# S5 outputs stored and fetched by GpSimd's queue, octaves 2 and 3 mixed behind more products

## The chip, the cores and the metric

The kernel runs on one NeuronCore of one Trainium2 chip. The metric is the device time of one execution in microseconds (us), lower is better; a kernel's time is the median over its runs. Engine names are those of the profile: PE is TensorE (matmuls), PEld its weight loads, DVE is VectorE, ACT is ScalarE, POOL is GpSimd, SP is SyncE. SPq and POOLq are the instruction queues of SP and POOL from which DMAs are issued.

## What is computed

One encoder layer over 512 tokens of width 1024, in float32. The part that matters here is the parallel mixer: an S5 state-space branch and a gMLP branch, merged by gates.

```python
xa, zu, zv = proj[..., :512], proj[..., 512:1536], proj[..., 1536:2560]
gate_a, gate_b = sigmoid(proj[..., 2560:3584]), sigmoid(proj[..., 3584:])
y  = d * u + s5_scan(u, forward) + s5_scan(u, backward)   # 32 groups of 16 channels, 64 states
y  = gelu(y)
ya = y * sigmoid(y @ w_glu)                               # 512 x 512
yb = gelu(zu) * spatial_mix(layer_norm(gelu(zv)))
merged = gate_a * (ya @ w_proj_a) + gate_b * (yb @ w_proj_b)
h = h + merged @ w_out
# then memory cross-attention and a SwiGLU feed-forward, unchanged here
```

## The kernel before

Each float32 product is made of three matmuls on a rounded high part and a remainder (`mm3`): high by high, low by high, high by low. A weight block of 512 KB is loaded by SP into a raw buffer (`wraw`, three buffers), rounded by ACT into `whi` (line 85) and subtracted by DVE into `wlo` (line 86), three buffers each. `next_w` takes the blocks in the order of a plan; it starts loads three blocks ahead and splits two blocks ahead. The raw buffer is free when `wlo` is written, and SP's next load waits for that.

The products with `w_proj_b` (`b_product`, line 1158) follow a scheme of seven half-size products for each half n of the columns, so fourteen blocks are used, each with 24 matmuls. They are written out by hand in lines 1223 to 1275, in accumulators `bx`, `bq`, `x1` and their copies (`seed`, `kept`). In the text, product (n, q) is product q of half n.

The S5 branch is a side program. Its 32 groups form four octaves of eight groups. `s5_outputs(o)` copies the scanned states of octave o to `ss`, and after a while `mix_` runs 24 matmuls, 48 records in the trace, into `py` (line 948): taps `tt` by inputs `u`, and output matrices `e` by states `ss`. DVE copies `py` to `yn` (957), PE transposes it to `pyt` (963), and DVE copies that to `y` (968). The matrices of octaves 2 and 3 were spilled to DRAM earlier (`ed`, `kd`) and are fetched back when the mix of octave o-2 is done (`reload`): SP loads `e` (867), POOL's queue loads `tt` (860).

How far such a step is put behind the one before it is set with `later(n, fn)`: `tick(us)` after each product counts work in units of 5.2 us, and what is due is then emitted. The emitted program is then ordered by a scheduler with a cost model; instructions marked `in_order` keep their place.

`store_outputs(n)` takes up to n finished octaves: ACT applies the gelu to `y` in place (980), and two DMAs for each octave write `y` to the DRAM scratch `yd[o]` (983), transposing its layout. After product (1,6) the S5 pool is closed; the pool `merge` takes its place, and a small memset `pad` on POOL (line 130) is the first to write there, so it waits for all users of the old pool. Then `ygt` is loaded from `yd` (1262), split into `yg_hi` on ACT (1263) and `yg_lo` on DVE (1264), and after the last two products the product with `w_glu` (`pf<-yg_hi` in line 360) begins.

Of the kernel before, what the change touches and what calls it, by code (L numbers as in the profile page):

```python
# [9 lines left out]
F32 = mybir.dt.float32  # L10
F32R = mybir.dt.float32r
AF = mybir.ActivationFunctionType
ALU = mybir.AluOpType
# [39 lines left out]
def hybrid_layer_kernel(  # L53
# [8 lines left out]
    nc = tc.nc  # L62
# [14 lines left out]
    def bank(name):  # L77
        return pm.tile([P, 512], F32, tag="mm", name=name)

    def aux(name, shape=(P, 512)):  # L80
        return pa.tile(list(shape), F32, tag="aux", name=name)
# [11 lines left out]
    in_order = tc.keep_in_program_order  # L93
# [349 lines left out]
    def later(n, fn):  # L443

        side["later"].append((side["now"] + n, fn))
# [171 lines left out]
    yd = [dp.tile([GO * C, Q, NCH], F32, name=f"yd{o}") for o in range(NO)]  # L617
# [163 lines left out]
    def lc(t, g):  # L781
        return t[:, g].rearrange("p a b -> p (a b)")
# [70 lines left out]
    ed = {o: dp.tile([2, P, GO * Q * C], F32, name=f"ed{o}") for o in (2, 3)}  # L853
# [10 lines left out]
    def reload(o):  # L864
        es = [s5p.tile([P, GO, Q, C], F32, tag="e%d" % i, name="e%d" % i, bufs=2) for i in range(2)]
        for i, e in enumerate(es):
            nc.sync.dma_start(glc(e), ed[o][i])
        load(o, es)
# [56 lines left out]
    def s5_outputs(o):  # L925
        gs = slice(o * GO, (o + 1) * GO)
        while ("oct", o) not in st:
            yield None
        e_re, e_im, tt = st["oct", o]
        zh, u = st["zh"], st["u"]  # L930
        ss = s5p.tile([P, 2, GO, NCH], F32, tag="wt", name="ss", bufs=2)
        zv = zh[:, :, :, gs].rearrange("p n i g -> p i g n")
        nc.gpsimd.memset(ss[lo_, :, :, 0:1], 0.0)
        nc.gpsimd.memset(ss[hi_, :, :, NCH - 1:NCH], 0.0)
        nc.scalar.copy(ss[lo_, :, :, 1:NCH], zv[lo_, :, :, 0:NCH - 1])
        V.tensor_copy(ss[hi_, :, :, 0:NCH - 1], zv[hi_, :, :, 0:NCH - 1][:, :, :, ::-1])

        def mix_():
            ps = aux("py", (P, 4, 2, 4, C))
            ks = (0, 1, 2) if o in ed else (1, 2, 0)  # L940
            for h in range(4):
                for k in ks:
                    for j in range(2):
                        g = 4 * j + h
                        a = u[:, o * GO + g, :] if k == 0 else ss[:, k - 1, g, :]
                        b = (lc(e_re, g), lc(e_im, g))[k - 1].rearrange("p (d q c) -> p d q c", d=2, q=4) if k else \
                            tt[:, h].rearrange("p (d q j c) -> p j d q c", d=2, q=4, j=2)[:, j]
                        in_order(nc.tensor.matmul(ps[64 * j:64 * j + 64, :, :, h, :].rearrange("p q d c -> p d q c"), a,
                                                  b, start=k == ks[0], stop=k == ks[2], tile_position=(0, 64 * j)))
            later(1, lambda: emit(ps))  # L950
            if o + 2 in ed:
                later(0.5, lambda: reload(o + 2))

        def emit(ps):

            y = s5p.tile([P, 512], F32, tag="etmp", name="yn")
            V.tensor_copy(y, ps.rearrange("p q d g c -> p (q d g c)"))
            later(0.5, lambda: turn_y(y))

        def turn_y(y):  # L960
            ps = aux("pyt", (P, 2, 4, NCH))
            for q in range(4):
                in_order(nc.tensor.transpose(ps[:, :, q, :], y[:, q * P:(q + 1) * P], ident))
            later(0.5 if o else 1.5, lambda: put(ps))

        def put(ps):
            y = s5p.tile([P, 512], F32, tag=("y", "bbr", "bbi", "raw_b")[o], name="y")
            V.tensor_copy(y, ps.rearrange("p s q n -> p (s q n)"))
            st["ys"].append((o, y))

        later(1, mix_)
        yield 5.0

    st["ys"] = []
# [1 line left out]
    def store_outputs(n):  # L976

        ready, st["ys"] = st["ys"][:n], st["ys"][n:]
        for o, y in ready:
            in_order(nc.scalar.activation(y, y, AF.Gelu_apprx_tanh))  # L980
            ydo = yd[o].rearrange("(s f) (d q) n -> d f s (q n)", s=2, d=2)
            for d in range(2):
                nc.sync.dma_start(ydo[d], y[64 * d:64 * d + 64].rearrange("p (s r) -> p s r", s=2))

    def s5_program():
        yield from s5_setup()
        for o in (2, 3):
            yield from s5_kernels(o)
        while "u" not in st:
            yield None  # L990
        zh = s5p.tile([P, NCH, 2, G], F32, name="zh")
        st["zh"] = zh
        for o in range(NO):
            yield from s5_inputs(o)
        for o in (0, 1):
            yield from s5_kernels(o)
        while st.get("nz", 0) < 2 * NO:
            yield None
        yield None
        yield from s5_scan()  # L1000
        for _ in range(2):
            yield None
        for o in range(NO):
            yield from s5_outputs(o)
# [161 lines left out]
    def unit_bank(name):  # L1166
        return bank(name).rearrange("p (j t) -> p j t", j=2)

    def seed(x):
        v = unit_bank("qv")  # L1170
        nc.scalar.copy(v, x)
        return v

    def kept(x, name):
        t = np_.tile([P, 2, 256], F32, tag="ev", name=name, bufs=2)
        nc.scalar.copy(t, x)
        return t

    def minus(x, t):
        nc.vector.tensor_tensor(t, x, t, ALU.subtract)  # L1180
        return t
# [17 lines left out]
    def last_sum(i):  # L1199
        k, lw, z0 = slice(2 * i, 2 * i + 2), slice(2 * i + 4, 2 * i + 6), zf[i][:, :, T0]  # L1200
        for yb_ in yb:
            nc.vector.tensor_tensor(z0, z0, yb_[:, lw, T0].bitcast(F32), ALU.add)
        split(bops[3][0][:, k], bops[3][1][:, k], z0)
# [14 lines left out]
    def gated(n, f, ts, src):  # L1218

        dst = part[:, 4 * n + 2 * f:4 * n + 2 * f + 2, ts]  # L1220
        nc.vector.tensor_tensor(dst, src, dst, ALU.mult)
# [7 lines left out]
    b_product(bv, 0, 2)  # L1229
    gated(0, 0, T0, bv)  # L1230
    store_outputs(2)
    b_product(bx, 0, 6)
    u2 = kept(bx, "u2")
    store_outputs(2)
    x1 = unit_bank("bx")
    b_product(x1, 1, 1, True)
    v1 = seed(x1)
    for i in range(2):
        last_sum(i)
    b_product(bx, 0, 7)  # L1240
    u3 = kept(bx, "u3")
    b_product(v1, 1, 2)
    gated(1, 0, T0, v1)
    gated(0, 1, T1, minus(bq, u3))
    b_product(bx, 0, 4)
# [3 lines left out]
    nc.scalar.copy(u1, x1)  # L1249
    finish_side()  # L1250
    store_outputs(NO)
    s5.close()
    mgx = ExitStack()
# [4 lines left out]
    yg_hi = mgp.tile([P, 4, T], F32R, name="yg_hi")  # L1258
    yg_lo = mgp.tile([P, 4, T], F32R, name="yg_lo")
    ygt = mgp.tile([P, 4, T], F32, name="ygt")  # L1260
    for m in range(4):
        nc.sync.dma_start(ygt[:, m, :], yd[m].rearrange("p l n -> p (l n)"))
        in_order(nc.scalar.copy(yg_hi[:, m, :], ygt[:, m, :]))
        nc.vector.tensor_tensor(yg_lo[:, m, :], ygt[:, m, :], yg_hi[:, m, :].bitcast(F32), ALU.subtract)
    b_product(bq, 0, 3)
    gated(0, 1, T0, minus(bq, u2))
    b_product(x1, 1, 7)
    u3 = kept(x1, "u3")
    bq = unit_bank("bq")
    b_product(bq, 1, 5, True)  # L1270
    gated(1, 1, T1, minus(bq, u3))
# [594 lines left out]
    for i in range(2):  # L1866
        p = aux("pcut", (P, 256))
# [37 lines left out]
```

## Time and profile before

| | |
|---|---|
| median of 3 runs | 874.87 us (873.5 to 876.44) |
| profiled execution: its own time | 879.31 us |
| its span, first to last instruction | 877.5 us |
| PE busy | 861.4 us of the span |
| DVE, ACT, POOL busy | 661.0, 464.9, 84.2 us |
| mean granted TensorE clock | 0.995 |
| DMA rate over the span | 193 GB/s moved by the core's 16 DMA engines |

Rows of the timeline give start, duration, engine, line, operation, output and inputs; in brackets stands the idle time of the engine before it and what ended that. A row of `xN` covers N instructions that follow each other. "To landing" is the time from the issue of a DMA until its semaphore shows it done. The profiled execution is one execution and lies above the three timed runs.

### The profile page before, as it was taken

How to read it: one execution, taken by the hardware profiler on the slowest of the kernel's cores; microseconds unless marked ns; L12 is line 12 of the kernel's file. 1: busy time of each engine (PE TensorE's matmuls, PEld its weight loads, DVE VectorE, ACT ScalarE, POOL GpSimd, SP SyncE). 2: the span in 40 equal slices, each digit the busy share in tenths (PEclk: the TensorE clock that was granted, in tenths of full speed). 3: DMA queues.
4: the chain of work that ended last, by engine and by line, in shares of the span. 5: the costliest groups of instructions: out<-in, count | busy, mean ns of one | idle time of the engine just before them, and what ended most of it. 6: DMA issues, size and time to landing. Idle time of an engine off the chain costs nothing.

```text
span 877.5 us, 14737 instructions
## 1 busy us (share of the span) xinstructions
PE 861.4 (98%) x5766; PEld 767.3 (87%) x5766; DVE 661.0 (75%) x1072; ACT 464.9 (53%) x693; POOL 84.2 (10%) x115
## 2 busy tenths in 40 slices
PE   7999999999999999999999999999999999999997
PEld 5787888888888988889899887999999999988885
DVE  5599895989846677658857746767878767899875
ACT  5543864144355553547556544645455454655674
POOL 1002100301020001100001001101111111000010
PEclk8999999999999999999999999999999999999999
DMA  8769656797653898736677546536899898366563
GB/s 243 191 164 293 132 156 179 170 251 193 168 168 95 271 310 253 248 107 208 202 236 220 133 124 169 164 126 171 226 238 224 218 240 217 97 181 212 195 229 107
DMA packets 116488, 169.56 MB, mean 193 GB/s; under 512 B 9265, under 2 KB 81473, under 8 KB 116290
## 3 DMA queue, kind: packets, MB, share of 16 engines
q1 hardware_dynamic: 96450, 140.59, 49.0%
q0 software_dynamic: 19680, 27.50, 19.7%
q8 instruction: 45, 0.74, 0.3%
q10 hardware_dynamic: 288, 0.52, 0.2%
q14 instruction: 25, 0.20, 0.1%
HBM read 159.71 MB, written 48.73 MB: 238 GB/s over the span
## 4 chain that ended last, share of the span: by engine, by line
PE 88%; DMA 6%; DVE 3%; ACT 1%; issue 1%; SPq 1%; ACTq 0%; DVEq 0%
PE pf L360 26%; PE pt L360 16%; PE px L1158 12%; PE pq L1158 6%; PE dx L360 5%; PE dq L360 3%; PE pv L1158 3%; PE qx L1158 2%; PE dv L360 2%; PE pz L892 2%; DMA wraw<-bsum 2%; DMA e<-ed 1%; PE psc L360 1%; PE ptr L520 1%; PE qq L1158 1%; DMA slab<-in_s_log_step_dram 1%
## 5 line engine op out<-in xcount | busy, mean ns | idle before, releaser
L85 ACT CAST whi<-wraw 128x1024 fp32r<-128x1024 f32 (+1 forms) x145 | 148.6, 1025 | 155.9 <-PE pf L360 54.7
L86 DVE TENSOR_TENSOR wlo<-wraw,whi 128x1024 fp32r<-128x1024 f32 (+1 forms) x145 | 172.1, 1189 | 61.1 <-ACT whi L85 60.5
L360 PE MATMUL pf<-xn,whi 128*128 128x512 f32 x448 | 140.3, 392 | 0.0
L360 PEld LDWEIGHTS pf<-xn,whi 128*128 128x128 f32 x448 | 83.7, 188 | 17.5 <-issue 0.4
L360 PE MATMUL pf<-xn,wlo 128*128 128x512 f32 x224 | 87.6, 392 | 0.0
L1158 PE MATMUL px<-fn,whi 128*128 128x256 f32 x480 | 83.3, 276 | 0.0
L1158 PEld LDWEIGHTS px<-fn,whi 128*128 128x128 f32 x480 | 72.5, 188 | 0.2
L86 DVE TENSOR_TENSOR wlo<-b,whi 128x1024 fp32r<-128x1024 f32 x40 | 48.9, 1223 | 26.0 <-ACT whi L85 25.9
L85 ACT CAST whi<-b 128x1024 fp32r<-128x1024 f32 x40 | 42.1, 1054 | 48.5 <-PE px L1158 27.4
L1158 PE MATMUL px<-fn,wlo 128*128 128x256 f32 x240 | 66.4, 277 | 0.0
L1158 PE MATMUL pq<-s,whi 128*128 128x256 f32 x320 | 55.0, 276 | 0.0
L360 PE MATMUL dx<-whi,s 128*128 128x512 f32 x166 | 52.2, 391 | 0.4 <-DVE h L1829 0.4
L86 DVE TENSOR_TENSOR wlo<-t,whi 128x1024 fp32r<-128x1024 f32 x30 | 36.7, 1225 | 18.4 <-ACT whi L85 18.4
L85 ACT CAST whi<-t 128x1024 fp32r<-128x1024 f32 x30 | 31.6, 1054 | 34.3 <-PE pv L1158 11.4
L360 PEld LDWEIGHTS pf<-xn,wlo 128*128 128x128 f32 x224 | 42.1, 188 | 8.7 <-issue 0.2
L1158 PEld LDWEIGHTS pq<-s,whi 128*128 128x128 f32 x320 | 48.2, 188 | 0.0
L360 PE MATMUL pt<-whi,xn 128*128 128x512 f32 x128 | 45.3, 421 | 2.4 <-ACT xn L85 2.1
L1158 PEld LDWEIGHTS px<-fn,wlo 128*128 128x128 f32 x240 | 45.1, 188 | 0.0
L1158 PE MATMUL pq<-s,wlo 128*128 128x256 f32 x160 | 44.2, 276 | 0.0
L360 PEld LDWEIGHTS dx<-whi,s 128*128 128x128 f32 x166 | 31.1, 188 | 7.4 <-issue 0.8
L360 PEld LDWEIGHTS pt<-whi,xn 128*128 128x128 f32 x128 | 25.0, 198 | 9.0 <-ACT xn L85 2.8
L360 PE MATMUL dx<-wlo,s 128*128 128x512 f32 x83 | 32.3, 391 | 0.0
(454 smaller groups left out, 2198.8 us busy)
## 6 DMA issues: line engine op xcount, KB each, us to landing
wraw<-in_w_in_dram SPq DMA_DIRECT2D x36, 512.0 KB, 4.6
dsum<-in_w_down_dram SPq DMA_DIRECT2D x20, 512.0 KB, 6.3
wraw<-dsum SPq DMA_DIRECT2D x20, 512.0 KB, 3.9
b<-in_w_gate_dram SPq DMA_DIRECT2D x15, 512.0 KB, 5.4
b<-in_w_up_dram SPq DMA_DIRECT2D x15, 512.0 KB, 5.3
wraw<-in_w_down_dram SPq DMA_DIRECT2D x15, 512.0 KB, 4.2
dsum<-in_w_down_dram POOLq DMA_DIRECT2D x10, 512.0 KB, 8.2
dsum<-dsum POOLq DMA_DIRECT2D x10, 512.0 KB, 8.0
```

The lines of the kernel that those rows point to most:

```text
L85: hi = nc.scalar.copy(dst_hi, src)
L86: lo = nc.vector.tensor_tensor(dst_lo, src, dst_hi.bitcast(F32), ALU.subtract)
L360: m = nc.tensor.matmul(ps, a[x], b[y], start=start and i == 0, stop=stop and i == 2, skip_group_check=free)
L520: m = nc.tensor.transpose(ps[:, j, :], src[:, k * P:(k + 1) * P], ident)
L892: nc.tensor.matmul(ps[:, g, :], wt[:, g, :], u[:, o * GO + g, :], start=True, stop=True)
L1158: nc.tensor.matmul(ps[:, j, :], a[x], b[y], start=start and j == k == i == 0, stop=k == 3 and i == 2, skip_group_check=True)
```

## The change

Four edits. The mix of octaves 2 and 3 is emitted 2.6 units after the copies to `ss`, not 1. The eight stores to `yd` and the four loads of `ygt` are issued by POOL's queue, not SP's. The second call of `store_outputs(2)` becomes two calls with one octave each, after the seed of product (1,1) and after product (1,2). The split of `ygt` into `yg_hi` and `yg_lo` is emitted after product (1,7), no longer right behind the loads.

```diff
-        later(1, mix_)
+        later(2.6 if o in ed else 1, mix_)
         yield 5.0
...
             for d in range(2):
-                nc.sync.dma_start(ydo[d], y[64 * d:64 * d + 64].rearrange("p (s r) -> p s r", s=2))
+                nc.gpsimd.dma_start(ydo[d], y[64 * d:64 * d + 64].rearrange("p (s r) -> p s r", s=2))
...
     u2 = kept(bx, "u2")
-    store_outputs(2)
     x1 = unit_bank("bx")
     b_product(x1, 1, 1, True)
     v1 = seed(x1)
+    store_outputs(1)
     for i in range(2):
         last_sum(i)
     b_product(bx, 0, 7)
     u3 = kept(bx, "u3")
     b_product(v1, 1, 2)
+    store_outputs(1)
...
     for m in range(4):
-        nc.sync.dma_start(ygt[:, m, :], yd[m].rearrange("p l n -> p (l n)"))
-        in_order(nc.scalar.copy(yg_hi[:, m, :], ygt[:, m, :]))
-        nc.vector.tensor_tensor(yg_lo[:, m, :], ygt[:, m, :], yg_hi[:, m, :].bitcast(F32), ALU.subtract)
+        nc.gpsimd.dma_start(ygt[:, m, :], yd[m].rearrange("p l n -> p (l n)"))
     b_product(bq, 0, 3)
     gated(0, 1, T0, minus(bq, u2))
     b_product(x1, 1, 7)
     u3 = kept(x1, "u3")
+    for m in range(4):
+        in_order(nc.scalar.copy(yg_hi[:, m, :], ygt[:, m, :]))
+        nc.vector.tensor_tensor(yg_lo[:, m, :], ygt[:, m, :], yg_hi[:, m, :].bitcast(F32), ALU.subtract)
```

The scheduler's order shows what this moves. On PE, before, the mix of octave 3 (`e_2664`, `e_2665`, with its `tt`) follows that of octave 2 at once, ahead of the last matmuls of the gate projection (`pf_2706`):

```order
L948 MATMUL py<-e_2588,ss 64x2x4x16 x2
L963 MATMUL pyt<-ident,yn 128x2x64 x4
L948 MATMUL py<-tt,u 64x2x4x16 x2
L948 MATMUL py<-e_2664,ss 64x2x4x16 x2
...
L948 MATMUL py<-e_2665,ss 64x2x4x16 x2
L360 MATMUL pf_2706<-xn,whi 128x512
```

On PE, in the change, at the same place (`bx` is product (0,1), `bq` product (0,5), `qv` product (0,2)):

```order
L948 MATMUL py<-e_2588,ss 64x2x4x16 x2
L1158 MATMUL bx<-yb_hi,whi 128x256
...
L1158 MATMUL bq<-s_2779,wlo 128x256
L948 MATMUL py<-tt,u 64x2x4x16 x2
L948 MATMUL py<-e_2664,ss 64x2x4x16 x2
...
L948 MATMUL py<-e_2665,ss 64x2x4x16 x2
L1158 MATMUL qv<-yb_hi,whi 128x256
```

All matmuls of the gate projection now stand ahead of octave 2's mix, and products (0,1) and (0,5) ahead of octave 3's. On SP, before, the stores and loads of the S5 outputs stand between the loads of the weight blocks (`bsum` holds sums of `w_proj_b` blocks):

```order
L226 DMA wraw<-bsum_81 128x1024
L983 DMA yd_254<-y 64x2x256 x2
L983 DMA yd_255<-y 64x2x256 x2
L226 DMA wraw<-in_w_proj_b_dram 128x4x256
...
L983 DMA yd_257<-y 64x2x256 x2
L226 DMA wraw<-in_w_proj_b_dram 128x4x256
L226 DMA wraw<-bsum_82 128x1024
L1262 DMA ygt<-yd_254 128x512
```

In the change these twelve stand on POOL, between the loads of the taps and the accumulating DMAs into `qsum`:

```order
L860 DMA tt<-kd_908 128x1x256 x4
L983 DMA yd_254<-y 64x2x256 x2
...
L983 DMA yd_257<-y 64x2x256 x2
L130 MEMSET pad 128x48
L1263 DMA ygt<-yd_254 128x512
...
L1263 DMA ygt<-yd_257 128x512
L277 DMA qsum_83<-in_w_q_dram 512x1x256
```

SP's weight loads now follow each other; SP also issues the last `w_proj_a` block and a copy into `qsum` ahead of the three `gat` loads, where they stood behind them. On ACT, before, the gelus come in two pairs and `yg_hi` ahead of three weight casts:

```order
L1176 COPY u_2963<-bx 128x512
L980 ACTIVATE y<-y 128x512 x2
L85 COPY whi<-wraw 128x1024
...
L1249 COPY zf<-bx 128x2x256
L1263 COPY yg_hi<-ygt 128x512 x4
L85 COPY whi<-wraw 128x1024 x3
L1176 COPY u_3222<-bx 128x512
```

On ACT, in the change (the first row is the seed of product (1,1), `u_3214` the copy after product (1,7)):

```order
L1171 COPY qv<-bx 128x512
L980 ACTIVATE y<-y 128x512
L85 COPY whi<-wraw 128x1024
L980 ACTIVATE y<-y 128x512
...
L85 COPY whi<-wraw 128x1024 x2
L1176 COPY u_3214<-bx 128x512
L1269 COPY yg_hi<-ygt 128x512 x4
L85 COPY whi<-wraw 128x1024 x3
```

The last gelu now stands behind one more weight cast, and `yg_hi` behind the casts of all weights of the `w_proj_b` products; the three casts behind it are two `w_glu` blocks and the first `w_proj_a` block.

## Prediction

> **What bounds the kernel now.** I read the page first, then the busy time by stages, then PE's timeline in the stage of the change.
>
> ```profile
> PE 861.4 (98%) x5766; PEld 767.3 (87%) x5766; DVE 661.0 (75%) x1072; ACT 464.9 (53%) x693; POOL 84.2 (10%) x115
> 250.00:272.00 22.00, 19.75 (x229) 16.55 (x224) 7.39 (x9) 6.60 (x6) 5.92 (x12) 1.00 0.70 193
> 272.00:314.00 42.00, 40.80 (x348) 39.70 (x346) 33.36 (x42) 27.26 (x37) 0.14 (x1) 1.00 0.67 207
> 314.00:352.00 38.00, 38.00 (x170) 31.44 (x169) 29.51 (x39) 16.55 (x23) 3.77 (x5) 1.00 0.94 283
> ```
>
> The first row gives busy time and share of the span, the others a stage, its length, the busy time of PE, PEld, DVE, ACT and POOL, the granted clock, the DMA share and rate. PE is the bound, busy 98% of the span, so only its gaps can be won. The granted clock is 1.00 in all three stages, so the gaps are waits and not a lower clock. The two stages that the change touches, 250 to 314 us, have 2.25 and 1.20 us without a matmul. That is less than what they lose, because ends of matmuls are modelled and a restart is slower. I therefore measure the loss from start to start.
>
> ```profile
> 249.57 0.66 PE L948 MATMUL py<-e,ss 128*64 128x128 f32 x8
> 254.96 0.66 PE L963 MATMUL pyt<-ident,yn 128*128 128x128 f32 x4
> 255.37 0.71 PE L360 MATMUL pf<-xn,whi 128*128 128x512 f32 x2
> ...
> 259.80 0.39 PE L360 MATMUL pf<-xn,whi 128*128 128x512 f32 x1
> 263.93 0.44 PE L948 MATMUL py<-tt,u 128*64 128x128 f32 x4 [0.36 <-DMA tt<-kd]
> 267.11 0.44 PE L948 MATMUL py<-e,ss 128*64 128x128 f32 x4 [1.13 <-DMA e<-ed]
> 269.45 0.50 PE L360 MATMUL pf<-xn,whi 128*128 128x512 f32 x1
> 272.07 0.60 PE L963 MATMUL pyt<-ident,yn 128*128 128x128 f32 x4
> ```
>
> Octaves 0 and 1 mix without waits: 249.57 to 254.96, 5.39 us for the pair, 2.70 each. A `pyt` takes 254.96 to 255.37, 0.41. Octaves 2 and 3 with one `pyt` run from 260.19 (259.80 + 0.39) to 269.45, 9.26 us. So they lose 9.26 - 5.39 - 0.41 = 3.5 us to reloads that have not landed, the last at 267.11.
>
> ```profile
> 278.43 0.28 PE L1158 MATMUL qv<-yb_hi,whi 128*128 128x256 f32 x1
> 305.60 0.39 PE L1158 MATMUL bq<-s,wlo 128*128 128x256 f32 x1 [0.62 <-DVE wlo L86]
> 308.38 2.72 PE bx L1158 x24
> 313.66 0.39 PE L360 MATMUL pf<-yg_hi,whi 128*128 128x512 f32 x1
> ```
>
> From 278.43, where product (0,2) starts, to the first `w_glu` matmul at 313.66 stand twelve products of 2.72 us, 32.6 us; 35.2 us pass. This stage loses 2.6 us to weights that are split late. SP's queue and its waits say why.
>
> ```profile
> SPq L983 <- ACT y L980: 4.2, 1, 4.2
> 277.57 0.32 SPq L226 DMA_DIRECT2D wraw<-bsum  x1
> 281.54 2.64 SPq L983 DMA_DIRECT2D yd<-y  x4
> 284.28 0.55 SPq L226 DMA_DIRECT2D wraw<-in_w_proj_b_dram  x1
> 272.04 2.18 ACT L85 CAST s<-zf 128x512 fp32r<-128x512 f32 x4 [11.45 <-PE pf L360]
> 284.78 1.15 ACT L980 ACTIVATE y<-y 128x512 f32<-128x512 f32 x2
> ```
>
> SP stands 4.2 us at the first store, waiting for a gelu, and issues no weight load between 277.57 and 284.28. And the weight chain starts late: ACT stands 11.45 us at the cast of `s` (it overwrites `xn`), until the last gate matmul, which is itself behind the late mixes.
>
> **Part 1, octaves 2 and 3 mixed later.** The order puts the last gate matmuls first. They and a `pyt` took 269.45 to 272.07 and 0.41 more, so octave 2 begins near 263.2 and reaches its fourth tap after three quarters of 2.70, at 265.2; that tap landed by 263.93. It ends at 265.9. Two products (5.4) later octave 3 begins at 271.4; its data landed by 267.11. Nothing waits: all 3.5 us are won. What is late next is product (0,5), which needs the casts of `s`: ACT can begin them at 263.2, 2.18 us, and DVE's half follows, ready before 267; the product starts at 268.6. Hidden; uncovered it would cost at most those 1.6 us.
>
> **Part 2, SP freed.** Octave 3 ends at 274.1, where product (0,2) starts, 4.4 us ahead of 278.43, with two `pyt` (0.8) still to come. The weight chain gains more: the gate matmuls end 8.9 us earlier and the SP wait is gone. Each block then needs a load, a cast and a subtraction:
>
> ```profile
> 290.58 1.05 ACT L85 CAST whi<-wraw 128x1024 fp32r<-128x1024 f32 x1 [1.03 <-DMA wraw<-bsum]
> 291.66 1.23 DVE L86 TENSOR_TENSOR wlo<-wraw,whi 128x1024 fp32r<-128x1024 f32 x1 [1.34 <-ACT whi L85]
> 295.95 7.21 DMA wraw<-bsum
> ```
>
> Even with the slow load of the chain's row, 7.21 + 1.05 + 1.23 = 9.5 us pass from a free raw buffer to a finished split. A raw buffer comes free 2.3 us (1.05 + 1.23) after the end of the product three blocks back, whose `whi` buffer the cast needs, and its next block is used three blocks on: 2.3 + 9.5 = 11.8 us, and five products are 13.6. It fits. I count the 2.6 us as won, less 0.6 for one wait of the size of that at 305.60 which may stay. The ends are nothing and 2.6; a loss is excluded, as SP's queue only loses work here.
>
> **Part 3, the way of the S5 outputs through POOL.** This is the added risk. The last gelu stands behind a weight cast that needs product (0,7)'s buffer. That product ends at 274.1 + 4 x 2.72 + 0.8 = 285.8; a cast (1.05) and a gelu (1.15 for two above, 0.58) give 287.4. Then come two stores, `pad`, four loads, `yg_hi`.
>
> ```profile
> 300.16 2.35 ACT L1263 CAST yg_hi<-ygt 128x512 fp32r<-128x512 f32 x4 [0.21 <-DMA ygt<-yd]
> L860 POOL DMA_DIRECT2D tt<-kd x8: 521/553/1026, 253.5 to 257.9; - x8
> DMA to landing us min/median/max: 2.5/7.7/9.8
> out_dram<-h POOLq DMA_DIRECT2D x2, 256.0 KB, 3.9
> out_dram<-rest POOLq DMA_DIRECT2D x2, 256.0 KB, 5.4
> yd<-y SPq DMA_DIRECT2D x8, 128.0 KB, 4.1
> ygt<-yd SPq DMA_DIRECT2D x4, 256.0 KB, 5.1
> ```
>
> A POOL issue is 0.55 us. For landing, no POOL row has this transfer. Low end: 3.9 us for each of the two steps, as `out_dram<-h`. High end: 9.8, the slowest `tt`, which ran beside four 512 KB loads of `e`. I take 5.4, since these transfers are issued between evenly spread weight loads. Last `ygt`: 287.4 + 2 x 0.55 + 5.4 + 0.1 + 4 x 0.55 + 5.4 = 301.6; with the ends, 298.6 and 310.4. Needed by: `w_glu` can start at 285.8 + 8 x 2.72 = 307.5. Before that stand a `yg_hi` (2.35 for four, 0.6) and two casts (1.05 each), so 304.8 is the latest. Covered by 3.2 us; at the high end it stalls 5.6.
>
> The Trainium skill ("DMA: Bandwidth & Descriptors", Specifications) gives about 1 us to the first byte for GpSimd's queue against 0.6 for SP's; by it, two steps at SP's 4.1 and 5.1 would be 0.8 later, an estimate that stays inside the cover. No run here shows that difference alone.
>
> POOL itself waits for nobody but these: `qsum`'s DMA behind them began at 317.54 in the trace. ACT, and through `yg_lo` DVE, would stand at a late `ygt`; queued there are the two `w_glu` casts and the subtraction that frees `bq` for product (1,3).
>
> ```profile
> 294.21 0.14 POOL L130 MEMSET pad<- 128x48 f32 x1 [35.77 <-DMA wraw<-in_w_proj_b_dram]
> 317.54 1.21 POOL L277 DMA_DIRECT2D qsum<-in_w_q_dram  x1 [23.19 <-DMA qsum<-qsum]
> 315.69 1.63 SPq L1297 DMA_DIRECT2D gat<-gad  x3
> 318.23 2.60 SPq L276 DMA_DIRECT2D qsum<-qsum  x1
> gat<-gad SPq DMA_DIRECT2D x4, 512.0 KB, 10.9
> 334.04 1.29 DVE L1301 TENSOR_TENSOR mg<-pf,gat 128x512 f32<-128x512 f32 x2 [4.74 <-PE pf L360]
> ```
>
> `gat` moves behind a weight load and the 2.60 us issue into `qsum`, about 4 us. Its landing at 315.69 + 10.9 = 326.6 was 7.4 us ahead of its use, where DVE waited for PE. Hidden, with 3.4 us left.
>
> **Sum.** 3.5 + 2.6 - 0.6 = 5.5 us. Against the profiled execution's 879.31 us that gives 873.8. It lies 4.4 above the median of 874.87; the same 5.5 off the median gives 869.4. PE stays gapless from 314 to 352, so the shift should reach the end.
>
> **Rivals.** *Late `ygt`.* Both POOL steps land like `tt`. A `ygt` between 304.8 and 310.4 takes back up to 5.6 us; half of that gives 872.2, all of it 874.9. For it: the median of 7.7 for landings of `tt`. Against it: 5.4 and 3.9 in the output stores.
>
> *POOL held by DVE: slower.* If DVE's work keeps POOL from writing descriptors, each of the six issues on the path takes longer.
>
> ```profile
> 653.68 1.43 POOL L277 DMA_DIRECT2D dsum<-dsum  x1
> 254.91 1.07 DVE L936 COPY ss<-zh 64x1008 f32<-64x1008 f32 x1 [0.84 <-issue]
> ```
>
> With the longest issue of the trace, 1.43, and landings of 9.8: 287.4 + 6 x 1.43 + 2 x 9.8 + 0.1 = 315.7. `w_glu` then starts 2.7 later at 318.4, not 313.66: 4.7 us slower, 879.6. It turns slower when `ygt` lands after 311.0. Against it: the eight `tt` issues ran beside DVE's SBUF copies (254.91) at a median of 553 ns. The Trainium skill ("SBUF — State Buffer", SBUF: two separate sides) warns that a fp32 SBUF copy in a two-port mode on VectorE locks GpSimd out of writing descriptors and says to issue from SP or ACT instead. The trace does not bear it out: at most 1026 ns in the eight issues.
>
> *Given back later.* From 314 to 352 the DMA engines are at a share of 0.94. If they set the pace there, a start 5.5 us earlier only waits longer: 874.9. Against it: PE had no gap there, and the loads are paced by freed buffers.
>
> *The change doesn't do what it says.* The waits at the mixes would stay if octave 3's data were later than 271.4; they landed by 267.11. Only part 2 would be left, 872.9.
>
> **Chances.** Forecast 0.70, own range 868.3 to 871.5; late `ygt` 0.11; POOL held or another slowdown 0.08; given back 0.07; waits stay 0.04. About 0.3% (2.6 us) is what a measurement of this kernel can tell from no change, so faster means under 872.2. The forecast and half of the late case are that: 0.76. Slower 0.08, and 0.16 between. The range is 867.5 to 874.9: the whole 6.1 us with some run spread (873.5 to 876.44 before) below, the late and given-back cases above.
>
> **What would show it.** Right: no waits of `py` on `tt` or `e`, product (0,2) some 4 us earlier, SP's loads without a hole, `yg_hi` not waiting for `ygt` beyond 304.8, `w_glu` starting near 308. Wrong: ACT standing at `yg_hi` for several us, or a POOL issue over 1 us, or new gaps of PE after 314.

## The result and the profile after

The changed kernel takes 871.18 us (median of 7 runs, 870.08 to 873.74), the kernel before 875.81 us in the same comparison (7 runs, 873.5 to 876.5). The ratio is 0.995, 95% interval 0.9939 to 0.9961: 3.4 to 5.3 us faster. The profiled execution of the changed kernel took 871.84 us, its span is 870.1 us. It is 7.5 us shorter than the profiled one of before, and one of the questions below is why that is more than the medians show.

First the page's row of busy times, then the busy times by stages, in the columns of the prediction:

```profile
PE 859.9 (99%) x5766; PEld 767.3 (88%) x5766; DVE 660.9 (76%) x1072; ACT 464.5 (53%) x693; POOL 92.3 (11%) x127
```
```profile
250.00:272.00 22.00, 22.00 (x237) 19.93 (x235) 16.23 (x21) 15.15 (x19) 5.92 (x12) 1.00 0.78 236
272.00:309.00 37.00, 37.00 (x319) 36.35 (x314) 25.52 (x31) 20.55 (x26) 7.26 (x13) 1.00 0.71 230
309.00:347.00 38.00, 38.00 (x170) 31.46 (x169) 28.95 (x39) 15.27 (x22) 3.77 (x5) 1.00 0.94 278
```

PE has no gap left in either stage (22.00 of 22.00 and 37.00 of 37.00), and none behind them at a DMA share of 0.94. PE's timeline shows the marks that the prediction named: octave 0, octave 2, octave 3, product (0,2), the first `w_glu` matmul.

```profile
247.67 0.66 PE L948 MATMUL py<-e,ss 128*64 128x128 f32 x8
261.18 0.44 PE L948 MATMUL py<-tt,u 128*64 128x128 f32 x4
269.60 0.44 PE L948 MATMUL py<-tt,u 128*64 128x128 f32 x4
272.38 0.39 PE L1158 MATMUL qv<-yb_hi,whi 128*128 128x256 f32 x1
306.14 0.39 PE L360 MATMUL pf<-yg_hi,whi 128*128 128x512 f32 x1
```

No `py` row has a wait in brackets any more. From octave 0 to `w_glu`, which I call the stage from here on, 58.47 us pass; before, 313.66 - 249.57 = 64.09. Octave 0 itself begins 1.9 us earlier than in the profile of before, ahead of all that was changed. From `w_glu` to the end of the span it is 563.96 us, before 563.84. So 5.6 of the 7.5 us are won in the stage, 1.9 ahead of it, and nothing is given back.

The S5 outputs on their new way, from the timelines of ACT and POOL:

```profile
261.06 2.18 ACT L85 CAST s<-zf 128x512 fp32r<-128x512 f32 x4 [2.36 <-PE pf L360]
285.43 0.63 ACT L980 ACTIVATE y<-y 128x512 f32<-128x512 f32 x1
286.35 1.20 POOL L983 DMA_DIRECT2D yd<-y  x2 [1.47 <-ACT y L980]
293.13 2.25 POOL L1263 DMA_DIRECT2D ygt<-yd  x4 [0.33 <-issue]
299.73 2.19 ACT L1269 CAST yg_hi<-ygt 128x512 fp32r<-128x512 f32 x4
```

And how long they took to land, from the rows of each line (the issues with their shortest, median and longest duration in ns, then the landing), `yd` first:

```profile
L983 POOL DMA_DIRECT2D yd<-y x8: 605/605/661, 272.9 to 286.9; - x8
DMA to landing us min/median/max: 3.1/3.6/4.3
L1263 POOL DMA_DIRECT2D ygt<-yd x4: 548/557/607, 293.1 to 294.8; - x4
DMA to landing us min/median/max: 4.3/4.7/6.0
```

ACT comes to `yg_hi` at 299.73 and does all four without a wait, so every `ygt` was there in time. The casts of `s` wait 2.36 us, not 11.45, and begin 11.0 us earlier (1.9 of them the earlier octave 0).

### The profile page after: what moved, and what is told of

It is laid out like the page before. It is cut to its first block, busy times and chain, and to the rows that moved or that the text cites. A ratio compares the mean times of both kernels' runs of the same rounds, so it can differ in the third digit from the quotient of the medians.

```text
span 870.1 us, 14734 instructions
## 1 busy us (share of the span) xinstructions
PE 859.9 (99%) x5766; PEld 767.3 (88%) x5766; DVE 660.9 (76%) x1072; ACT 464.5 (53%) x693; POOL 92.3 (11%) x127
## 4 chain that ended last, share of the span: by engine, by line
PE 95%; DMA 2%; DVE 1%; ACT 1%; SPq 1%; issue 0%; ACTq 0%; DVEq 0%
PE pf L360 26%; PE pt L360 16%; PE px L1158 13%; PE dx L360 6%; PE pq L1158 6%; PE dq L360 3%; PE pv L1158 3%; PE bx L1158 3%; PE qx L1158 3%; PE dv L360 2%; PE pz L892 2%; PE qv L1158 1%; PE po L360 1%; PE psc L360 1%; PE py L948 1%; PE qq L1158 1%
## 5 line engine op out<-in xcount | busy, mean ns | idle before, releaser
L277 POOL DMA_DIRECT2D dsum<-in_w_down_dram x12 | 13.3, 1109 | 174.7 <-DMA dsum<-in_w_down_dram 171.0
```

The source lines that it names most:

```text
L277: plan[j + step][1].append((0, lambda d=dst, x=more: nc.gpsimd.dma_start(d, x, accum_op=ALU.add)))
```

## The experiments

Part 1 to Part 3 are the prediction's. The edits are called *mix* (octaves 2 and 3 later), *queue* (stores and loads by POOL), *single stores* (two calls of `store_outputs(1)`) and *late split* (`yg_hi`, `yg_lo` behind product (1,7)). The first theory was the prediction's: mix wins 3.5 us, the queue 2, the other two only keep `ygt` out of the way. Each kernel gives a ratio to the kernel before and a profile. Since executions of one kernel spread by some 5 us (870.79 to 875.75 in a second set of the changed kernel), the stage in the profile separates the kernels better than the medians. It was 58.47 in both profiles of the changed kernel, 63.77 and 64.09 in those of before; the largest difference between two profiles of one kernel is 0.45 us.

| edits | stage, us | ratio to before, 95% |
|---|---|---|
| none | 64.09, 63.77 | (second run) 1.0 (0.9987 to 1.0014) |
| late split | 63.58 | 0.9994 (0.9979 to 1.001) |
| mix, queue, single stores | 62.97 | 0.9972 (0.9953 to 0.9991) |
| queue | 62.75 | 0.9987 (0.9968 to 1.0005) |
| queue, single stores, late split | 61.04 | 0.9973 (0.9954 to 0.9992) |
| all, delay 1.8 | 60.74 | 0.996 (0.9944 to 0.9975) |
| mix, single stores | 59.91 | 0.9962 (0.9944 to 0.998) |
| mix, single stores, late split | 58.96, 58.51 | 0.9965 (0.9948 to 0.9982), 0.9959 (0.9945 to 0.9973) |
| mix, late split | 58.47 | 0.9968 (0.9953 to 0.9983) |
| all | 58.47, 58.47 | 0.995 (0.9939 to 0.9961), 0.996 (0.9943 to 0.9977) |
| all, delay 3.4 | 58.58 | 0.9943 (0.9928 to 0.9958) |

**Each edit undone.** First the queue, from the changed kernel:

```diff
-                nc.gpsimd.dma_start(ydo[d], ...)
+                nc.sync.dma_start(ydo[d], ...)
-        nc.gpsimd.dma_start(ygt[:, m, :], yd[m].rearrange("p l n -> p (l n)"))
+        nc.sync.dma_start(ygt[:, m, :], yd[m].rearrange("p l n -> p (l n)"))
```

> The whole change but for the queue: stores to yd and loads of ygt stay with SP, mixes late, split of ygt late. Theory (two terms: 3.5 us from the order of the mixes, about 2 from SP no longer standing at the stores): the waits of py are gone, but SP stands again some 4 us at a store behind a gelu, and loads of weights come late; 3.5 us faster than the kernel before, not 4.6. Rival 1 (the order alone: the weight chain was late only because the gate matmuls ended 9 us late): as fast as the whole change, 4.6 us faster, PE without gaps. Rival 2 (the queue carries most): at most 1.5 us faster.

The stage was 58.96, only 0.5 us longer than with all edits. PE waited once, 0.2 us. That speaks for rival 1, the order alone; the ratio, 3.1 us faster than before, could not tell. The kernel was therefore run again later, beside a second run of the changed kernel on the same chip.

Second, the mixes put back to where they were:

```diff
-        later(2.6 if o in ed else 1, mix_)
+        later(1, mix_)
```

> The whole change but for the order of the mixes: octaves 2 and 3 are mixed as early as before. Theory: waits of py on tt and e return (9.3 us for the pair and a pyt), ACT stands 11 us at the casts of s; POOL's queue and the late split keep 1 to 2 us: 1 to 2 us faster than before. Rival 1: no difference, within 0.5 us. Rival 2: 3 us faster or more. If the late split of ygt is worth something by itself, it is faster than the kernel with only the queue.

The waits of `py` are back, 1.0 us for `e` and 0.9 for `tt` by the records. But from product (0,2), at 275.05, to `w_glu`, at 307.69, it takes 32.64 us, exactly twelve products of 2.72. So Part 2 can be won in full without Part 1. It is 2.4 us faster than before.

Third, the late split undone:

```diff
+        in_order(nc.scalar.copy(yg_hi[:, m, :], ygt[:, m, :]))
+        nc.vector.tensor_tensor(yg_lo[:, m, :], ygt[:, m, :], ...)
     b_product(bq, 0, 3)
...
     u3 = kept(x1, "u3")
-    for m in range(4):
-        in_order(nc.scalar.copy(yg_hi[:, m, :], ygt[:, m, :]))
-        nc.vector.tensor_tensor(yg_lo[:, m, :], ygt[:, m, :], ...)
```

> The whole change but for the late split: yg_hi stands on ACT right behind zf again, ahead of three weight casts. Theory: ygt lands near 300, ACT comes to yg_hi near 295, so ACT stands about 4 us, the weights of products (1,3) and (1,7) are cast late, and PE waits 1 to 3 us: 2 to 3.5 us faster than before, not 4.6. Rival (the cover is larger than I think, weights are two blocks ahead): as fast as the whole change, 4.6 us faster.

The stage was 62.97 us: of the 5.5 us won, 4.5 were gone. The timelines of ACT and PE, and then a row of the chain of waits, show the way it takes:

```profile
297.74 0.62 ACT L1264 CAST yg_hi<-ygt 128x512 fp32r<-128x512 f32 x1 [3.79 <-DMA ygt<-yd]
299.17 0.62 ACT L1264 CAST yg_hi<-ygt 128x512 fp32r<-128x512 f32 x1 [0.80 <-DMA ygt<-yd]
302.62 0.58 ACT L1176 COPY u<-bx 128x512 f32<-128x512 f32 x1
303.25 0.38 PE L1158 MATMUL bx<-yb_hi,whi 128*128 128x256 f32 x1 [2.60 <-ACT u L1176]
```
```profile
303.25 4.60 PE bx L1158 x24
```

ACT stands 4.6 us at `yg_hi`. The weight casts and the copy `u` are queued behind it, PE waits 2.60 us for the copy and then does a product in 4.60 instead of 2.72. The stand and the wait are the sizes I expected. The slow product is something else, as a row by stretches shows (the clock is the third number from the end):

```profile
303.20:307.60 4.40, 4.34 (x24) 4.35 (x25) 4.37 (x6) 0.95 (x2) 0.00 (x0) 0.63 0.65 203
```

The granted clock was 0.63 there. By its starts the product took 4.40 us; behind the shorter wait in the last kernel of this section, at a clock of 1.00, it took 2.84. So some 1.6 of the 4.5 us are the clock. In the 14 traces this is the only fall of the clock between 24 and 860 us, and it follows the longest wait of PE in any of the stages. Whether the wait caused it was not tried.

**The queue alone**, from the kernel before:

```diff
-                nc.sync.dma_start(ydo[d], ...)
+                nc.gpsimd.dma_start(ydo[d], ...)
-        nc.sync.dma_start(ygt[:, m, :], yd[m].rearrange("p l n -> p (l n)"))
+        nc.gpsimd.dma_start(ygt[:, m, :], yd[m].rearrange("p l n -> p (l n)"))
```

> Only the queue: stores to yd and loads of ygt by POOL, everything else as before. Theory: the 3.5 us of waits at the mixes of octaves 2 and 3 stay; the loss between product (0,2) and w_glu shrinks from 2.6 to 1 or 1.5, since the weight chain still starts late; 1 to 2 us faster than before. Rival 1 (the order alone): no difference, within 0.5 us. Rival 2 (the queue carries most): 3 us faster or more. A late ygt, with yg_hi ahead of weight casts on ACT, could turn it slower by 1 to 3 us.

The stage won 1.0 to 1.3 us; the ratio says 1.1 us faster, with no difference inside its interval. So 1 to 2 us holds at its low end. ACT stood 0.8 and 0.2 us at `yg_hi`, and PE's wait for `wlo` was gone. From product (0,2) to `w_glu` 34.29 us pass, 1.65 more than twelve products of 2.72. By the starts of single matmuls only 0.8 of that are stops of PE, where the kernel before has 2.5; the rest is products at a slower pace (see the end). So the queue alone takes away more of the stops than the stage's length shows.

**The late split alone.** The edits with queue and late split but without mix won 1.7 us more than the queue alone, so the late split seemed a term of its own.

```diff
-        in_order(nc.scalar.copy(yg_hi[:, m, :], ygt[:, m, :]))
-        nc.vector.tensor_tensor(yg_lo[:, m, :], ygt[:, m, :], ...)
...
     u3 = kept(x1, "u3")
+    for m in range(4):
+        in_order(nc.scalar.copy(yg_hi[:, m, :], ygt[:, m, :]))
+        nc.vector.tensor_tensor(yg_lo[:, m, :], ygt[:, m, :], ...)
```

> Only the late split: yg_hi and yg_lo behind product (1,7), everything else as before. New theory (the late split is a term of its own: before, ACT does yg_hi ahead of three weight casts, and 12 products take 35.2 us instead of 32.6): from product (0,2) to w_glu about 33.5 us, 1.5 to 2 us faster than before. My theory of the prediction (the loss there came from SP standing at the stores, the late split only guards against a late ygt): no difference, within 0.5 us.

This new theory fell. From product (0,2) to `w_glu` it is 34.82 us, 0.4 less than before, and the ratio is 0.9994. Some 0.5 of it is the slower pace; PE's stops are down only from 2.5 to 1.7 us. Without `yg_hi` in its way ACT waits longer for the load, as its timeline shows:

```profile
296.07 0.59 ACT L1249 COPY zf<-bx 128x512 f32<-128x512 f32 x1 [0.79 <-PE bx L1158]
299.33 1.05 ACT L85 CAST whi<-wraw 128x1024 fp32r<-128x1024 f32 x1 [2.67 <-DMA wraw<-bsum]
```

So with the mixes early, two things follow each other on the way of a weight, the load and `yg_hi`. Taking `yg_hi` away leaves most of the stops; taking SP's stand away (the queue alone) leaves a third.

**The kernel before once more**, with no edit, for the 1.9 us ahead of the stage.

> The kernel before, unchanged, for a second profile. If the 1.9 us by which octave 0 began earlier in the changed kernel came from the change, octave 0 begins near 249.6 here too; if they are scatter of single executions ahead of the stage, it begins anywhere from 246.5 to 249.6. The stage from octave 0 to w_glu should again be near 64 us, and from there to the end 563.8.

Here are the first rows of octave 0 and of `w_glu` on PE's timeline in that second profile, then the same two in a second profile of the changed kernel (the run with the changed kernel unchanged, below):

```profile
246.44 0.66 PE L948 MATMUL py<-e,ss 128*64 128x128 f32 x8
310.21 0.39 PE L360 MATMUL pf<-yg_hi,whi 128*128 128x512 f32 x1
```
```profile
250.75 0.66 PE L948 MATMUL py<-e,ss 128*64 128x128 f32 x8
309.22 0.39 PE L360 MATMUL pf<-yg_hi,whi 128*128 128x512 f32 x1
```

The stages, 63.77 and 58.47, repeat. The start of octave 0 does not: 249.57 and 246.44 before, 247.67 and 250.75 after. The 1.9 us were scatter between single executions; over all 14 profiles octave 0 began from 246.35 to 250.75. Most of it comes from the first 24 us. Here is the stretch from 16 to 24 us in the first profile of before, then of the changed kernel:

```profile
16.00:24.00 8.00, 6.40 (x21) 5.10 (x22) 4.41 (x11) 2.42 (x7) 1.10 (x2) 0.79 0.84 213
16.00:24.00 8.00, 6.85 (x38) 5.64 (x36) 4.88 (x12) 3.10 (x10) 1.10 (x2) 1.00 0.82 217
```

At a granted clock of 0.79 PE did 21 matmuls, at 1.00 it did 38. The clock was 0.79 there in three profiles, the first of before, the second of the changed kernel and that of mix with single stores; their octave 0 began at 249.57, 250.75 and 250.18. In the other eleven it was 1.00, and octave 0 began from 246.35 to 248.66. From 24 us to octave 0 PE is busy without a gap in all of them.

**The size of the delay.** From the changed kernel, first 1.8, then 3.4:

```diff
-        later(2.6 if o in ed else 1, mix_)
+        later(1.8 if o in ed else 1, mix_)
```

> The changed kernel with a delay of 1.8 units instead of 2.6: octave 2 stands where it stood before, ahead of the last gate matmuls, octave 3 right behind them. Theory (the mixes lose what their data lacks when they begin): octave 2 waits for its taps again and loses about 1.7 us, octave 3 loses nothing: 1.7 us slower than the changed kernel, about 3 us faster than before. Rival (any delay that parts the two octaves is enough): as fast as the changed kernel.

The stage was 60.74, 2.3 us longer than with 2.6. Octave 2 again waited for its taps; by the starts it took 3.82 us (257.17 to 260.99) instead of 2.77, 1.05 lost. The rest, about 1.2 us, is no wait: its products take 2.83 us each instead of 2.72 (see the end). The theory holds, but for a smaller term.

> The changed kernel with a delay of 3.4 units instead of 2.6: each mix one or two products later. The mixes have no waits either way. Theory: the last gelu comes up to 2.7 us later, ygt lands near 303, still ahead of 304.8: no difference to the changed kernel, within 0.5 us. Rival (the cover of ygt is thinner than worked out): ACT stands at yg_hi, 1 to 3 us slower than the changed kernel.

The stage was 58.58 and the ratio 0.9943, no difference. But it did not try the cover of `ygt`: the last gelu came 37.9 us after octave 0, as with 2.6 (37.8), because a weight cast holds it and not the mix.

**Queue and stores once the order is right.** The last four ran on one chip. First the changed kernel without an edit, then with the queue undone by the diff above:

> The changed kernel, unchanged, beside the next one on the same chip. From octave 0 to w_glu again 58.5 us; 4.6 us faster than before.

> Again the whole change but for the queue (stores and loads of the S5 outputs by SP). If POOL's queue is worth only the 0.5 us that the two profiles show (stage 58.96 against 58.47), it is within 1 us of the changed kernel. If it is worth the 1.5 us that separate medians suggest, it is 1 to 2 us slower, and the stage must show it.

The stage was 58.47 with the queue and 58.51 without; the medians were 872.83 and 872.28 us. So these two runs show no worth of POOL's queue; the first run without it (58.96) shows 0.5 us. In both profiles without it ACT waits for two weight loads (3.84 and 0.43 us in the first, 3.17 and 0.64 in the second), which SP issues behind the loads of `ygt`. In the changed kernel its casts there wait for PE. The weights come just in time by SP's queue: in the first run the last of these casts began 0.45 us later after octave 0 than in the second, and the stage was 0.45 us longer.

Then the single stores were undone too, so that only mix and late split were left (from the kernel with the queue undone):

```diff
     u2 = kept(bx, "u2")
+    store_outputs(2)
...
     v1 = seed(x1)
-    store_outputs(1)
...
     b_product(v1, 1, 2)
-    store_outputs(1)
```

> Mixes late and split of ygt late, but stores by SP and in two pairs (store_outputs(2) in its old place). In the order the last gelu then falls behind zf on ACT, and the loads of ygt behind the first w_glu block on SP. Theory (the two single stores are part of the gain, since they keep ygt ahead of its use): ygt lands after 304.8, w_glu waits, 3 to 6 us of the gain are lost: between as fast as before and 2 us slower or faster. Rival (the store edits cost and bring nothing): as fast as with single stores, 3 to 4 us faster than before.

The theory fell: stage 58.47, PE without a wait. The last gelu did come 8.5 us later (293.94), and the last `ygt` only just before 304.24:

```profile
293.94 0.63 ACT L980 ACTIVATE y<-y 128x512 f32<-128x512 f32 x1
295.23 1.05 ACT L85 CAST whi<-wraw 128x1024 fp32r<-128x1024 f32 x1 [0.66 <-PE bq L1158]
298.18 1.05 ACT L85 CAST whi<-wraw 128x1024 fp32r<-128x1024 f32 x1 [1.89 <-PE bx L1158]
304.24 0.62 ACT L1268 CAST yg_hi<-ygt 128x512 fp32r<-128x512 f32 x1 [0.76 <-DMA ygt<-yd]
306.02 0.39 PE L360 MATMUL pf<-yg_hi,whi 128*128 128x512 f32 x1
```
```profile
SPq L983 <- ACT y L980: 6.9, 3, 3.3
```

The first rows are from the timelines of ACT and PE, the last is from SP's waits (total, times, longest). SP stood 6.9 us at the stores, more than the 4.2 of before, and nothing was late: the two weight casts ended their wait on PE, not on a load. In this order of the stores the weights are far enough ahead to take it. I put that down to the gate matmuls, which end 9 us earlier. It is shown only together with the late split, since the late mixes alone were not run.

Last, mix and single stores without queue and late split; both are undone from the changed kernel by the diffs shown above:

> Mixes late and single stores, but by SP's queue and with the split of ygt early, behind zf on ACT. With POOL's queue that lost 4.5 us, because ygt landed 3.8 us after ACT came to it. By SP's queue the loads of ygt begin 2.85 us earlier after octave 0. Theory (what counts is when ygt lands against ACT at yg_hi): ACT stands about 1 us, some 2 us of the gain are lost, about 2.5 us faster than before. Rival (the early split costs 4 us whatever the queue): no faster than before.

The sizes came about as expected: ACT stood 1.4 us, 1.4 us of the gain in the stage were lost, and by the ratio it is 3.3 us faster. The rival, no gain with the early split, is out. The loads of `ygt` by each queue, first by POOL (mix, queue, single stores), then by SP, with who stood at them (us, times) and their landing times:

```profile
L1263 POOL DMA_DIRECT2D ygt<-yd x4: 546/556/607, 292.3 to 294.0; - x4
  ACT yg_hi L1264: 4.6, 2
DMA to landing us min/median/max: 5.2/6.4/6.9
```
```profile
L1263 SPq DMA_DIRECT2D ygt<-yd x4: 325/428/634, 293.0 to 294.6; - x4
  ACT yg_hi L1264: 1.4, 1
DMA to landing us min/median/max: 3.8/4.5/5.2
```

Octave 0 began at 247.46 and 250.18 in these two, so POOL issued the first load 44.9 us after it and SP 42.8. By POOL they started 2.0 us later and took 1.9 longer, ACT stood 4.6 and not 1.4 us, and the stage is 62.97, not 59.91. So with the mixes late and the split early, the one profile with POOL's queue is 3.1 us longer, of which some 1.6 are the fallen clock. The ratios, 0.9972 and 0.9962, do not tell the two apart.

But in the SP kernel the stand at `ygt` is not what PE waited for. ACT's rows, PE's wait and the load from the chain:

```profile
299.18 1.23 ACT L1264 CAST yg_hi<-ygt 128x512 fp32r<-128x512 f32 x2 [1.36 <-DMA ygt<-yd]
301.44 1.05 ACT L85 CAST whi<-wraw 128x1024 fp32r<-128x1024 f32 x1 [1.03 <-DMA wraw<-bsum]
302.94 1.05 ACT L85 CAST whi<-wraw 128x1024 fp32r<-128x1024 f32 x1 [0.45 <-DMA wraw<-in_w_proj_b_dram]
304.52 0.38 PE L1158 MATMUL bx<-yb_hi,whi 128*128 128x256 f32 x1 [1.15 <-ACT u L1176]
```
```profile
295.50 7.34 DMA wraw<-in_w_proj_b_dram
```

After `yg_hi` ACT waits twice more, for two weight loads that SP issued behind the loads of `ygt`. The last cast began 52.76 us after octave 0, against 51.36 in the second run with SP's queue and the late split: 1.40 us later, and the stage is 1.40 us longer. So the loss here is a late weight, and what the early split itself costs by SP's queue is not shown.

## Why the prediction was right, and where not

**Part 1, octaves 2 and 3 mixed later: right.** From octave 0 to product (0,2) it was 28.86 and 28.57 us before and is 24.71 after. Two `pyt` of 0.35 by their starts now come behind that mark, so 25.4: won are 3.2 to 3.5, counted were 3.5. Taking off the 1.9 us of the earlier start, the forecasts for octaves 2 and 3 and product (0,2) become 261.3, 269.5 and 272.2; measured are 261.18, 269.60 and 272.38. The casts of `s` were hidden, as said. The delay of 1.8 shows that it is not the parting of the octaves but when the data lands that counts.

**Part 2, SP freed: right in size, wrong in cause.** From product (0,2) to `w_glu`, without the two `pyt`, 33.76 - 0.70 = 33.06 us pass, against 35.2: won are 2.2, counted were 2.0. What failed is the step that gave it to SP's queue, on top of the earlier weight chain. With SP still doing all stores and loads the stage is nearly or just as short (58.96 and 58.51, and 58.47 with SP standing 6.9 us). The late mixes and the late split together are enough: the weight chain begins 9 us earlier and can take SP's stand. Neither shows it without the other: the late split alone takes 34.82 us, mix with single stores 35.21 - 0.70 = 34.51. The step was right for the kernel with the mixes early: there the queue alone takes 1.7 of 2.5 us of PE's stops, and 2.7 to 3.0 us of the stage go with the queue, late split and single stores together; what the single stores do in that without the queue was not tried. Nor was what remained "one wait" of 0.6: PE has no wait left. Of the 0.4 us over twelve products, 0.2 are in product (0,2), which took 2.93 us by its starts (272.38 to 275.31), and 0.1 each in two products that stand behind a `pyt`; the other nine took 2.72.

**The step that excluded a loss rests on the late split.** I wrote that SP's queue "only loses work here". That held for SP, but the loads on POOL land later, and with the split where it was before, ACT stands at them. The prediction did not price the late split at all. It is what makes the queue harmless: without it the stage is 4.5 us longer in the one profile, 2.9 if the fallen clock is taken off.

**Part 3, the way through POOL: right.** The last gelu ended at 286.1 (forecast 287.4, less 1.9: 285.5). A POOL issue took 0.56 to 0.61 us, landings 3.6 and 4.7 us where I took 5.4. No `ygt` was later than `yg_hi`'s end at 301.9; the forecast for the last was 301.6, needed by 304.8; with the earlier start, 299.7 and 302.9. The bound was too tight. With only mix and late split, where octave 0 began at 247.55, it would be 302.8; the last `ygt` landed just before 304.24, 1.4 us later, and `w_glu` still started in time. The bound counted both `w_glu` casts ahead of the product; one had been done between two `yg_hi`, and the other began at 305.81, only 0.2 us ahead of `w_glu`'s start. `gat` landed in 11.3 to 13.7 us, and DVE still waited for PE at its use:

```profile
326.53 1.29 DVE L1303 TENSOR_TENSOR mg<-pf,gat 128x512 f32<-128x512 f32 x2 [4.57 <-PE pf L360]
```

**The rivals.** *Late `ygt`* did not happen in the changed kernel, but it did as soon as the late split was undone. *Given back later*: 563.96 us behind the stage, 563.84 and 564.09 before; no. *POOL held by DVE* did not happen either: the longest of the twelve issues was 661 ns. But the prediction read its evidence against it wrongly. Of the eight `tt` issues only one ran beside a copy of DVE into `ss`, and that is the one of 1026 ns; the other seven took 0.52 to 0.57 us. It ended 0.14 us after the copy. The changed kernel repeats it, with 0.12 us:

```profile
253.02 1.07 DVE L936 COPY ss<-zh 64x1008 f32<-64x1008 f32 x1 [0.84 <-issue]
253.19 1.02 POOL L860 DMA_DIRECT2D tt<-kd  x1
```

In all 14 traces that issue took 1.02 to 1.03 us. This agrees with the warning of the Trainium skill ("SBUF — State Buffer", SBUF: two separate sides) that certain VectorE copies keep GpSimd from writing descriptors. The twelve new issues had no such copy beside them: from 272.9 to 295.4 DVE's only copies are `yn` and `y`, which read matmul outputs. So the rival stayed away because of where the issues stand, not because such copies are harmless.

**The sum.** 5.5 us were forecast; the stage shows 5.3 to 5.6. The medians moved by 4.6 us in the first set and 3.4 in the second (intervals 3.4 to 5.3 and 2.0 to 5.0). Of the 1.8 us by which 871.18 lies above the forecast of 869.4, 0.9 is the median of before, which was 875.81 in that comparison instead of 874.87; the other 0.9 is this difference between stage and medians. It stays open. Without the three profiles whose clock fell between 16 and 24 us, octave 0 begins from 246.35 to 246.65 in the four with the mixes early, 246.49 on average, and from 246.84 to 248.66 in the six with a delay of 2.6 or more, 247.51 on average. That 1.0 us is about what the medians lack. But PE's order is the same in all of them up to there, so the change gives no reason for it; it may be chance, and the runs do not settle it.

## What to carry to other kernels

Undo each edit of a change by itself before giving it credit: here mix and late split by themselves reach the whole gain in the stage, and the move to POOL's queue adds nothing to them there and loses where the late split is missing. A wait in a queue costs only what its consumers lack in lead; shorten the chain ahead of them first and look again. When a stage is longer, follow the wait that ended last and look at the granted clock before an edit gets the blame. A wait that merely has the expected size may not be the cause. An instruction that stands in an in-order engine for a transfer should come behind all work that others need sooner.

## What the runs showed of the hardware

The same 24 matmuls (128x128 by 128x256) take 2.72 us in one stretch and 2.83 in another, without a wait and at a granted clock of 1.00. The chains of the changed kernel and of the one with delay 1.8, from the same products:

```profile
284.55 2.72 PE qv L1158 x24
287.27 5.44 PE bx L1158 x48
295.65 2.72 PE bx L1158 x24
```
```profile
284.91 2.83 PE qv L1158 x24
287.74 5.65 PE bx L1158 x48
296.45 2.83 PE bx L1158 x24
```

From matmul to matmul that is 0.113 us in one stretch and 0.118 in the other. In the changed kernel product (0,2) has the slower pace, and from 276 us on everything the faster one. With delay 1.8 the slower pace holds from 270 us to `w_glu`, with the queue alone from 286.5 on, behind a stop of PE, and with the late split alone from 290.7 to 302.0, between two stops. In these traces the pace changed only within half a microsecond of a stop or of matmuls of another shape. It makes 1.3, 0.9 and 0.5 us in these three kernels, as much as some of the edits. What sets it was not tried. Apart from the pace, the first matmul behind a `pyt` takes 0.20 us to the next and behind a wait 0.22 to 0.23.

Transfers by POOL's queue landed no slower than by SP's in the changed kernel (`yd` 3.6 against 4.1, `ygt` 4.7 against 5.1 before), but in another order of the same work `ygt` took 6.4 by POOL and 4.5 by SP. The landing time of a queue was not a constant here. What POOL's queue did show is that an issue beside a copy of DVE from SBUF to SBUF took 1.02 us instead of 0.55.
